# V from x·g with its rows scaled by the root afterwards, in a one-core decoder-layer kernel

## The chip, the core and the metric

The kernel runs on one core of a Trainium2 chip. The metric is the device time of one execution in microseconds. A core has TensorE (PE, with its weight loads PEld), VectorE (DVE), ScalarE (ACT), GpSimd (POOL) and SyncE (SP). Each works through its own instructions in the order of the program and waits on semaphores for the others. Here SP issues nearly all of the loads.

## What is computed

One layer of a decoder trunk, for one sequence of 1024 tokens of width 1024, in float32. Only the first sub-layer matters here:

```
mod = silu(c) @ w_ada + b_ada                        # shift, scale, gate (two sub-layers)
u   = (x * rsqrt(mean(x*x) + EPS)) * g_mix * (1 + scale) + shift
q, k, v, us, g_att, g_ssm = split(u @ w_in)
o_att = softmax over the dilated windows of q k^T, times v     # rows of the softmax sum to 1
...                                                  # S5 branch, gates, projection, conv MLP, final norm
```

Write g for g_mix·(1 + scale), one number for each channel, and r for the root rsqrt(...), one number for each token. Then u = r·(x·g) + shift, and u @ W = r·((x·g) @ W) + shift @ W.

## The kernel before, in words

Every float32 product is made of three matmuls on rounded halves: `mm3` (lines 182 to 186) multiplies high by high, high by low and low by high. A "split" writes the high half on ACT (a rounding copy) and then the low half on DVE (the difference). The work is laid out channel block by channel block, k = 0 to 7, 128 channels each; token halves are called hf = 0 and 1, 512 tokens each.

Stage one (lines 330 to 449) loads x transposed (`xs[k]`), the rows of w_ada that give the scale, and the first weights `w0`; DVE makes scale k with one row dot product (`row_dot`), ACT and DVE write x·g as two halves into a page `xg[k]`, and PE accumulates seven products of `w0` with xg in seven PSUM buffers `b0` (q and k of the first pair of heads and the inputs of the S5 branch). Meanwhile x is also loaded by tokens (`xn`), ACT sums its squares, and eight more row dots give the shift. `root` (line 388) makes r; `spread_a`, `spread_b` (lines 399 and 404) spread it over all partitions as `rr` with one matmul for each token half.

Between the stages (lines 452 to 507) PE multiplies the shift by `w0` (16 narrow matmuls, L488 and L489), and `u_half` begins to write u into new pages: for one k and one half, `u_a` is L1437 on DVE (x·g·r, in place in `xs`) and L1438 on ACT (high half of u), and `u_b` is L1443 on DVE (low half). `scale_r` (L462) multiplies the products in PSUM by rr and moves them into SBUF (`t0`).

Stage two (lines 566 to 609) makes v: for hf, for k, four token tiles t, one `mm3` each, with u as the stationary operand and w_v (`wv`, split by `split_w`, lines 301 to 306) as the moving one; eight PSUM buffers `vps`, four for each half. In the second half, around each k, DVE and ACT also turn `t0` into q and k of the first heads (`put_q`, `put_k`) and the finished first-half tiles into V (`put_v`: four copies L525 on ACT, four differences L528 on DVE). After the last product come `put_v(4)` to `put_v(7)`; the buffers `mm` that `put_v(4)` and `put_v(5)` read are the ones in which the next stage's first products are accumulated. The next stage is attention, with the remaining products of u as filling work for PE; before its first exponential, ACT copies the S5 inputs (L562) and loads its table.

The order on each engine is written by hand. `Builder` keeps a clock that `b.unit` moves on after each product; generators handed to `b.spawn` are resumed when that clock has passed the time that they last yielded, in the order in which they were spawned. `b.drain` runs them to their ends. `Weights` prefetches weight items the same way: its split is L118 on ACT and L121 on POOL.

## Time and profile before

| | before |
|---|---|
| median of 3 runs | 1157.44 us (1157.3 to 1157.76) |
| the profiled execution's own time | 1157.34 us |
| its span, first to last instruction | 1155.4 us |
| mean granted clock of TensorE | 0.986 |
| PE busy | 1112.6 us, 96% |
| DVE busy | 872.6 us, 76% |
| ACT busy | 581.8 us, 50% |

The span is the profiler's; the time of an execution is 1.94 us longer than it. The busy share of an engine is an average over stages that have different limits: what a change in one stage is worth is read from that stage's own timeline and waits.

### The profile page before, as it was taken

Reading aid. Unit: us, or ns where it says so; the run is one execution under the profiler, and the core shown is the slowest. Engines: PE = TensorE matmul, PEld = TensorE weight load, DVE = VectorE, ACT = ScalarE, POOL = GpSimd, SP = SyncE. Lnnn points to the kernel's source line nnn. Section 1 sums busy time; section 2 is a strip of 40 time slices with the busy share of each in tenths; the row PEclk is TensorE's granted clock in tenths of the full one; section 3 lists DMA queues with packets and bytes.
Section 4 is the critical chain, followed back from the end, with each engine's and each line's share of the span. In section 5 each row is a group of like instructions: output and inputs, shape, how many; then the busy total and the mean of one; then the engine's idle time right before and its main releaser. Section 6 shows DMA issues by size and latency. Waiting matters only on the chain.

```text
span 1155.4 us, 14755 instructions
## 1 busy us (share of the span) xinstructions
PE 1112.6 (96%) x5286; PEld 917.2 (79%) x5286; DVE 872.6 (76%) x1672; ACT 581.8 (50%) x1062; POOL 150.2 (13%) x171
## 2 busy tenths in 40 slices
PE   9899999999999999999799998999999999999995
PEld 8677888888878887888688886788888888887884
DVE  6678687876568597378767779888877768889777
ACT  3648777778732312242334565452445346736653
POOL 1001444545421312000000000000000000000003
PEclk9899999999999999999899999999999999999997
DMA  9811111111022221146592342255424337779333
GB/s 370 343 55 70 49 38 37 56 37 65 17 75 73 57 87 51 64 140 195 166 381 81 120 201 73 91 175 190 143 76 146 109 109 272 257 293 343 129 126 146
DMA packets 57337, 159.20 MB, mean 138 GB/s; under 512 B 7440, under 2 KB 13712, under 8 KB 55472
## 3 DMA queue, kind: packets, MB, share of 16 engines
q1 hardware_dynamic: 47520, 144.56, 35.1%
q10 hardware_dynamic: 9744, 13.70, 3.7%
q8 instruction: 41, 0.67, 0.2%
q14 instruction: 32, 0.26, 0.1%
HBM read 126.20 MB, written 31.46 MB: 136 GB/s over the span
## 4 chain that ended last, share of the span: by engine, by line
PE 66%; DVE 15%; ACT 8%; DMA 7%; issue 3%; POOL 0%; SPq 0%; DVEq 0%; ACTq 0%
PE ps_s L1305 13%; PE ps_mm L1305 10%; PE ps_t L1305 8%; PE ps_mm L184 6%; PE ps_mm L185 6%; PE ps_mm L186 6%; PE ps_s L186 3%; PE ps_s L184 3%; PE ps_s L185 3%; DMA xn<-in_xn 2%; PE ps_t L1598 2%; PE ps_s L1562 1%; PE ps_o L1615 1%; PE ps_s L1563 1%; DMA wraw<-in_w 1%
## 5 line engine op out<-in xcount | busy, mean ns | idle before, releaser
L1305 PE MATMUL ps_s<-op,half 128*128 128x512 f32 x792 | 189.5, 390 | 3.0 <-ACT ps_s L1319 2.4
L1305 PEld LDWEIGHTS ps_s<-op,half 128*128 128x128 f32 x792 | 148.4, 188 | 35.4 <-ACT ps_s L1319 3.8
L184 PE MATMUL ps_mm<-u,whl 128*128 128x512 f32 x360 | 145.0, 403 | 3.1 <-ACT sg L737 2.0
L186 PE MATMUL ps_mm<-u,whl 128*128 128x512 f32 x360 | 141.6, 393 | 0.0
L185 PE MATMUL ps_mm<-u,whl 128*128 128x512 f32 x360 | 141.4, 393 | 0.0
L1305 PE MATMUL ps_mm<-op,half 128*128 128x512 f32 x528 | 126.9, 393 | 3.0 <-DVE f L1010 2.8
L1305 PEld LDWEIGHTS ps_mm<-op,half 128*128 128x128 f32 x528 | 99.7, 189 | 24.6 <-ACT half L1110 3.2
L1305 PE MATMUL ps_t<-op,half 128*128 128x512 f32 x432 | 103.9, 390 | 0.7 <-ACT tp L1313 0.7
L1305 PEld LDWEIGHTS ps_t<-op,half 128*128 128x128 f32 x432 | 81.0, 188 | 17.9 <-ACT tp L1313 1.1
L1407 POOL TENSOR_TENSOR hh<-hh,acc 128x512 f32<-128x512 f32 x3 | 4.2, 1439 | 652.1 <-DVE acc L1432 652.1
L121 POOL TENSOR_TENSOR whl<-wraw,whl 128x256 fp32r<-128x256 f32 (+2 forms) x52 | 62.0, 1193 | 207.8 <-ACT whl L118 207.8
L184 PEld LDWEIGHTS ps_mm<-u,whl 128*128 128x128 f32 x360 | 68.1, 189 | 15.3 <-ACT sg L737 2.5
L186 PEld LDWEIGHTS ps_mm<-u,whl 128*128 128x128 f32 x360 | 68.0, 189 | 15.3 <-DVE whl L121 0.3
L185 PEld LDWEIGHTS ps_mm<-u,whl 128*128 128x128 f32 x360 | 68.3, 190 | 10.5
L1603 DVE TENSOR_TENSOR PT<-ps_t,PT 128x512 fp32r<-128x512 f32 (+1 forms) x80 | 50.6, 633 | 28.2 <-ACT PT L1601 27.7
L1111 DVE TENSOR_TENSOR half<-scr,half 128x512 fp32r<-128x512 f32 x80 | 54.5, 685 | 16.2 <-ACT half L1110 16.1
L118 ACT ACTIVATE whl<-wraw 128x256 fp32r<-128x256 f32 (+2 forms) x73 | 49.7, 681 | 28.3 <-PE ps_s L186 14.6
L1574 ACT ACTIVATE S<-S,mcol 128x128 f32<-128x128 f32 (+3 forms) x64 | 49.3, 771 | 14.5 <-DVE mcol L1572 13.0
L1578 POOL TENSOR_SCALAR S<-S,mcol 128x128 f32<-128x128 f32 (+3 forms) x64 | 48.6, 761 | 49.9 <-DVE mcol L1577 35.9
L1110 ACT ACTIVATE half<-scr 128x512 fp32r<-128x512 f32 x80 | 49.0, 626 | 8.6 <-DVE scr L1092 5.5
L1111 DVE TENSOR_TENSOR half<-wraw,half 128x512 fp32r<-128x512 f32 x66 | 45.0, 686 | 7.6 <-ACT half L1110 7.5
L1601 ACT ACTIVATE PT<-ps_t 128x512 fp32r<-128x512 f32 (+1 forms) x80 | 43.7, 550 | 10.4 <-PE ps_t L1598 9.3
(507 smaller groups left out, 2438.0 us busy)
## 6 DMA issues: line engine op xcount, KB each, us to landing
wraw<-in_wup SPq DMA_DIRECT2D x32, 512.0 KB, 3.7
fq<-f SPq DMA_DIRECT2D x16, 1024.0 KB, 5.4
ft<-fq SPq DMA_DIRECT2D x14, 1024.0 KB, 7.5
ada<-in_wada SPq DMA_DIRECT2D x24, 512.0 KB, 8.7
wraw<-in_wdn SPq DMA_DIRECT2D x20, 512.0 KB, 5.9
adaB<-in_wada ACTq DMA_DIRECT2D x16, 512.0 KB, 4.9
wraw<-in_wout SPq DMA_DIRECT2D x16, 512.0 KB, 3.9
hd<-h SPq DMA_DIRECT2D x12, 512.0 KB, 7.9
```

What stands on the lines that cost most here:

```text
L118: nc.scalar.activation(w[:, 0, cs], raw[:, cs], AF.Copy)
L121: lo.tensor_sub(w[:, 1, cs], raw[:, cs], w[:, 0, cs].bitcast(F32))
L184: nc.tensor.matmul(ps, wh, xh, start=first, stop=False)
L185: nc.tensor.matmul(ps, wh, xl, start=False, stop=False)
L186: nc.tensor.matmul(ps, wl, xh, start=False, stop=last)
L1110: nc.scalar.activation(w[:, 0], src, AF.Copy)
L1111: lows.append(lambda: nc.vector.tensor_sub(w[:, 1], src, w[:, 0].bitcast(F32)))
L1305: mm = lambda wp, xp, i: nc.tensor.matmul(ps, w[:, wp, ws], xp[:, cs], start=first and k + i == 0, stop=k == KT // 2 - 1 and i == 2, skip_ ...
L1574: nc.scalar.activation(tl, tl, AF.Exp, bias=mc[:, 0:1], scale=-1.0, accum_out=mc[:, 2:3])
L1578: nc.gpsimd.tensor_scalar(tl, tl, mc[:, 3:4], 0.0, op0=OP.mult, op1=OP.add)
L1601: nc.scalar.activation(pt[:, 0, :w], tps[:, :w], AF.Copy)
L1603: 0, lambda: nc.vector.tensor_sub(pt[:, 1, :w], tps[:, :w], pt[:, 0, :w].bitcast(F32)))
```

## The change

v is made of x·g instead of u: the second stage multiplies the pages `xg` that stage one left, so it needs no root; each row of the result is multiplied by r when it leaves PSUM (`put_v` takes it, from a new third row of `ssq`, as the scale of its copies and of its differences, which become `scalar_tensor_tensor`). The shift's part, shift @ w_v, is a constant row for each head; it is made by a second run of 16 narrow matmuls (`rows_of("v", wv)`) and eight small transposes, kept as `vb`, and added to the attention's output behind the softmax (line 1627's add becomes a `scalar_tensor_tensor` with that column).

u is still needed by the later products. It now takes the place of x·g in the same pages: `gen_u`, in the background, writes u for (k, hf) once the products of that k and half have been given (`taken`). The seven first products are copied out of PSUM on ACT as they end (`keep`) and scaled in SBUF later. Six of the eight row dots for the shift and their loads, the spreading of the root, and the shift's row for `w0` are moved into the second stage; the first w_v load and split are moved ahead into the first. `put_q`, `put_k` and `put_v` are spawned instead of being run in place.

```diff
...
@@ -50,7 +50,8 @@
 EPS = 1e-6
 BIG = 1e30
 WARM = 31
-DOTS = ((4, 5), (5, 1), (5, 4), (6, 0), (6, 2), (6, 4), (6, 6), (7, 1))
+DOTS = ((7, 1), (7, 4))
+U_PACE = 1.5
...
         def split_w(i):
             raw = raws.pop(i)
-            w = b.whl.tile([P, 2, 1024], R32, name="whl", tag="whl") if i == 5 else b.A([P, 2, 1024], R32, "whA")
+            w = b.whl.tile([P, 2, 1024], R32, name="whl", tag="whl") if i == 7 else b.A([P, 2, 1024], R32, "whA")
...
         def load_xn(n):
-            if n in (0, 2):
+            if n % 2 == 0:
                 page = b.A([P, 2, D], F32, "xn")
                 xnp[n], xnp[n + 1] = page[:, 0], page[:, 1]
-            nc.sync.dma_start(xnp[n % 4], I["xn"][n])
+            nc.sync.dma_start(xnp[n], I["xn"][n])
 
         def square(n):
 
-            nc.scalar.activation(xnp[n % 4], xnp[n % 4], AF.Square, accum_out=ssq[:, 0, n:n + 1])
+            x = xnp.pop(n)
+            nc.scalar.activation(x, x, AF.Square, accum_out=ssq[:, 0, n:n + 1])
...
+            nc.vector.tensor_scalar(ssq[:, 2], r, -1.0, None, op0=OP.mult)
...
+        def keep(i, ps):
+            if not t0_pages:
+                t0_pages.extend(b.A([P, 4, HF], F32, "t0") for _ in range(2))
+            t0[i] = t0_pages[i[0] // 2][:, 2 * (i[0] % 2) + i[1]]
+            nc.scalar.activation(t0[i], ps, AF.Copy)
+
         late = {}
-        for fn, at in ((row_dot, DOTS), (root, ((7, 0),)), (spread_a, ((7, 2),))):
+        for fn, at in ((row_dot, DOTS), (root, ((7, 2),))):
             for a, kn in enumerate(at):
                 late.setdefault(kn, []).insert(0, (fn, a))
...
-            if 3 <= k < 7:
-                load_row(2 * k - 6)
-                load_row(2 * k - 5)
-            if 2 <= k < 6:
-                for n in (2 * k - 4, 2 * k - 3):
-                    if n > 3:
-                        square(n - 4)
-                    load_xn(n)
+            for n in {2: (0, 1), 3: (2, 3), 4: (4, 5), 5: (6, 7)}.get(k, ()):
+                load_xn(n)
+            for n in {4: (0, 1), 5: (2, 3), 6: (4, 5)}.get(k, ()):
+                square(n)
+            if k == 5:
+                load_w(4)
+            for n in {5: (0, 1), 6: (2, 3)}.get(k, ()):
+                load_row(n)
             if k + 1 < KT:
                 prep_b(k + 1)
             if k + 2 < KT:
                 prep_a(k + 2)
             elif k == 6:
-                for n in range(4, KT):
+                for n in (6, 7):
                     square(n)
-                load_w(4)
+                wv = [split_w(4)]
                 load_w(5)
             o = (k % 2) * 512
             for n, ((t, hf), ps) in enumerate(b0.items()):
@@ -443,23 +455,23 @@
                 for fn, a in late.get((k, n), []):
                     fn(a)
                 b.mm3(ps, w[:, 0], w[:, 1], xg[k][:, 0, halves[hf]], xg[k][:, 1, halves[hf]], k == 0, k == KT - 1)
+                if k == KT - 1:
+                    keep((t, hf), ps)
                 b.unit(0.65)
-            del xg[k]
-        spread_b(0)
+        b0.clear()
+        del ps
         b.drain()
...
+        t0_pages.clear()
+        u = [xg[k] for k in range(KT)]
+        xg.clear()
 
         def scale_r(*ii):
             for i in ii:
-                nc.vector.tensor_mul(t0[i], b0.pop(i), rr[:, halves[i[1]]])
+                nc.vector.tensor_mul(t0[i], t0[i], rr[:, halves[i[1]]])
...
-        def u_half(k, hf, *between):
-            u_a(k, hf)
-            scale_r(*between)
-            u_b(k, hf)
...
+        taken = set()
+
+        def gen_u():
+
+            last = None
+            for hf in range(2):
+                for k in range(KT):
+                    while (k, hf) not in taken:
+                        yield 0.6
+                    u_a(k, hf)
+                    if last:
+                        u_b(*last)
+                    if last and last[1]:
+                        xs[last[0]] = None
+                    last = k, hf
+                    yield U_PACE
+            yield 0.7
+            u_b(*last)
+            xs[last[0]] = None
+
...
+        def shift():
+            nc.vector.tensor_add(mod[:, 0:KT], mod[:, 0:KT], cols[:, 0:KT])
+            nc.vector.tensor_copy(shl[:, :, 0], mod[:, 0:KT])
+            nc.vector.tensor_sub(shl[:, :, 1], mod[:, 0:KT], shl[:, :, 0].bitcast(F32))
+
+        def rows_of(n, ws, tag="o"):
+
+            ps = b.ps(tag)
+            for k in range(KT):
+                o = (k % 2) * 512
+                w = ws[k // 2][:, :, o:o + 512]
+                nc.tensor.matmul(ps[0:2], shl[:, k], w[:, 0], start=k == 0, stop=False)
+                nc.tensor.matmul(ps[0:1], shl[:, k, 0:1], w[:, 1], start=False, stop=k == KT - 1)
+                b.unit(0.43)
+            brow[n] = b.tp()
+            nc.scalar.activation(brow[n][0:2], ps[0:2], AF.Copy)
...
@@ -522,10 +549,11 @@
                 V.extend(b.A([P, 8, 2, P], R32, "V") for _ in range(4))
             src = vps[t].rearrange("p (h d) -> p h d", h=8)
             for p in range(4):
-                nc.scalar.activation(V[p][:, t, :, 0:HD], src[:, 2 * p:2 * p + 2], AF.Copy)
-            yield
+                nc.scalar.activation(V[p][:, t, :, 0:HD], src[:, 2 * p:2 * p + 2], AF.Copy, scale=ssq[:, 2, t:t + 1])
+            yield 0.7
             for p in range(4):
-                nc.vector.tensor_sub(V[p][:, t, :, HD:P], src[:, 2 * p:2 * p + 2], V[p][:, t, :, 0:HD].bitcast(F32))
+                nc.vector.scalar_tensor_tensor(V[p][:, t, :, HD:P], src[:, 2 * p:2 * p + 2], ssq[:, 2, t:t + 1],
+                                               V[p][:, t, :, 0:HD].bitcast(F32), op0=OP.mult, op1=OP.subtract)
...
         for hf in range(2):
             for k in range(KT):
                 if hf == 0:
-                    if k % 2 == 0 and k < 6:
-                        wv.append(split_w(5 + k // 2))
-                        if k == 0:
-                            load_w(7)
-                    if 1 < k + 1 < KT:
-                        u.append(b.A([P, 2, S], R32, "u"))
-                        u_half(k + 1, 0, *{3: [(1, 1)], 4: [(2, 1)], 5: [(0, 1)]}.get(k, []))
                     if k == 0:
+                        load_w(6)
+                        load_row(4)
+                        load_row(5)
+                        spread_a(0)
+                        row_dot(2)
+                        row_dot(3)
+                        wv.append(split_w(5))
+                    if k == 1:
+                        load_w(7)
+                        load_row(6)
+                        load_row(7)
+                        spread_b(0)
                         spread_a(1)
-                    if k == 1:
+                        row_dot(4)
+                        scale_r((1, 0))
+                        row_dot(5)
+                    if k == 2:
                         spread_b(1)
+                        wv.append(split_w(6))
+                        row_dot(6)
+                        scale_r((2, 0))
+                        row_dot(7)
+                        shift()
+                        b.spawn(gen_u(), 0.5)
+                    if k == 3:
+                        scale_r((0, 0))
+                    if k == 4:
+                        rows_of("u", w0)
+                        w0.clear()
+                        wv.append(split_w(7))
                     if k == 5:
-                        bias_cols()
+                        scale_r((3, 0), (1, 1))
+                        bias_cols("u", P, bias0)
+                    if k == 6:
+                        scale_r((2, 1))
+                        rows_of("v", wv)
                     if k == 7:
-                        u_half(0, 1)
-                        u_a(1, 1)
+                        scale_r((0, 1))
+                        bias_cols("v", HD, vb)
                 else:
                     if k == 0:
                         qk_tiles(0)
+                    if k in (2, 4):
+                        wv[k // 2 - 1] = None
                     put = put_q(0, k, add_bias0(0, k)) if k < 2 else put_k(0, k - 2, add_bias0(1, k - 2)) if k < 4 \
                         else put_v(k - 4)
-                    if k + 1 < KT:
-                        u_b(k + 1, 1)
-                    next(put)
-                    if k + 2 < KT:
-                        u_a(k + 2, 1)
-                    list(put)
-                    xs[k] = None
+                    b.spawn(put)
                     if k == 3:
                         us0 = [(t - 2, hf, add_bias0(t, hf)) for t, hf in ((2, 0), (2, 1), (3, 0))]
                     if k in (3, 6):
...
                     b.mm3(vps[t], u[k][:, 0, t * P:(t + 1) * P], u[k][:, 1, t * P:(t + 1) * P],
                           wv[k // 2][:, 0, o:o + 512], wv[k // 2][:, 1, o:o + 512], k == 0, k == KT - 1)
                     b.unit(0.65)
+                taken.add((k, hf))
             if hf == 0:
                 del xnp
                 vps += [b.ps(t) for t in ("mm", "mm", "o", "o")]
+        b.drain()
+        for t in range(4, 8):
+            list(put_v(t))
         p1.close()
         wv = None
         p2 = ExitStack()
...
         W.prefetch(1)
-        for t in range(4, 8):
-            list(put_v(t))
         for x in us0:
...
             hp = slice(64 * h2, 64 * h2 + 64)
             nc.scalar.activation(t[0:64, 0:256], o[64:128, 0:256], AF.Copy)
-            nc.vector.tensor_add(t[hp, 256:512], o[0:64, 0:256], t[0:64, 0:256])
+            nc.vector.scalar_tensor_tensor(t[hp, 256:512], o[0:64, 0:256], vb[0:64, 2 * p + h2:2 * p + h2 + 1], t[0:64, 0:256],
+                                           op0=OP.add, op1=OP.add)
             oo = Oat[p][hp, :, 2 * j * P:(2 * j + 2) * P]
```

## Rows read from the trace of the kernel before

**Rows 1.** The page, part 1: busy us, share of the span and instructions of each engine.

```profile
PE 1112.6 (96%) x5286; PEld 917.2 (79%) x5286; DVE 872.6 (76%) x1672; ACT 581.8 (50%) x1062; POOL 150.2 (13%) x171
```

**Rows 2.** Timeline of PE: start, us, line, operands, idle before with its releaser.

```profile
48.88 0.39 PE L186 MATMUL ps_o<-xg,whA 128*128 128x512 f32 x1
...
54.01 2.08 PE L407 MATMUL ps_o<-tp,nones 128*128 128x512 f32 x2 [4.74 <-ACT tp L402]
56.77 0.59 PE L488 MATMUL ps_o<-whl,shl 128*2 128x512 f32 x1 [0.69 <-ACT rr L408]
...
58.65 0.39 PE L489 MATMUL ps_o<-whl,shl 128*1 128x512 f32 x1
...
61.20 0.40 PE L184 MATMUL ps_s<-whA,u 128*128 128x512 f32 x1
...
65.48 1.02 PE L407 MATMUL ps_o<-tp,nones 128*128 128x512 f32 x2
...
77.32 0.40 PE L504 MATMUL ps_o<-ident,tp 2*128 2x2 f32 x4
...
108.33 0.39 PE L186 MATMUL ps_o<-whA,u 128*128 128x512 f32 x1
109.83 0.47 PE L184 MATMUL ps_mm<-u,whl 128*128 128x512 f32 x1 [1.10 <-DVE V L528]
```

**Rows 3.** Chain of work that ended last, first 55 us: start, us, what.

```profile
40.24 8.93 DMA xn<-in_xn
...
52.68 1.29 ACT tp L402 x4
```

**Rows 4.** Stretches: us, busy time (instructions) by engine, clock, DMA share, GB/s.

```profile
86.00:108.72 22.72, 22.24 (x97) 17.74 (x95) 20.11 (x41) 18.91 (x45) 3.73 (x2) 1.00 0.06 23
...
130.00:330.00 200.00, 196.85 (x1178) 168.68 (x1177) 139.91 (x407) 149.89 (x327) 93.22 (x124) 1.00 0.14 44
```

**Rows 5.** Timeline of DVE.

```profile
59.50 0.69 DVE L462 TENSOR_TENSOR t<-ps_s,rr 128x512 f32<-128x512 f32 x1
...
92.41 0.75 DVE L1437 SCALAR_TENSOR_TENSOR xk<-xk,gs,rr 128x512 f32<-128x512 f32 x1
93.08 0.67 DVE L551 TENSOR_TENSOR KL<-t,KH 64x512 fp32r<-64x512 f32 x1
...
94.47 0.42 DVE L555 CAST KH<-KH 64x512 fp32r<-64x512 f32 x1
...
101.80 1.54 DVE L1443 SCALAR_TENSOR_TENSOR u<-x,mod,u 128x512 fp32r<-128x512 f32 x1
...
108.00 0.89 DVE L528 TENSOR_TENSOR V<-ps_t,V 128x128 fp32r<-128x128 f32 x4 [1.65 <-ACT V L525]
108.80 1.67 DVE L528 TENSOR_TENSOR V<-ps_mm,V 128x128 fp32r<-128x128 f32 x8
```

**Rows 6.** Timeline of ACT.

```profile
9.50 0.61 ACT L379 ACTIVATE whl<-wvx 128x512 fp32r<-128x512 f32 x1
10.02 0.71 ACT L318 ACTIVATE xg<-xk,gs 128x512 fp32r<-128x512 f32 x1
...
100.23 0.74 ACT L525 ACTIVATE V<-ps_s 128x128 fp32r<-128x128 f32 x4
100.85 0.73 ACT L1438 ACTIVATE u<-x,mod 128x512 fp32r<-128x512 f32 x1
...
113.26 1.23 ACT L562 ACTIVATE usr<-t 128x512 f32<-128x512 f32 x1 [0.43 <-ACT usr L562]
```

**Rows 7.** Timeline of POOL.

```profile
100.41 2.39 POOL L121 TENSOR_TENSOR whl<-wraw,whl 128x1024 fp32r<-128x1024 f32 x1 [95.26 <-ACT whl L118]
```

**Rows 8.** Timeline of SP, the queue that issues the loads.

```profile
42.85 0.33 SPq L298 DMA_DIRECT2D wvx<-in_wv  x1
44.09 0.33 SPq L298 DMA_DIRECT2D wraw<-in_wv  x1
```

**Rows 9.** Line 1627 alone: its instructions, min/median/max ns, first and last start.

```profile
L1627 DVE TENSOR_TENSOR tp<-ps_o,tp x32: 406/417/419, 132.0 to 325.0; 64x256 f32<-64x256 f32 x32
```

More of the change, by code (lines that the diff above doesn't have):

```diff
@@ L566, in body @@
         vps = [b.ps(t) for t in ("s", "s", "t", "t")]
+        puts = []
         for hf in range(2):
@@ L687, in body @@
         W.slow = True
-        attention(b, V, QK, Oat, pS, near, far, ident, mcol, fill)
+        attention(b, V, QK, Oat, pS, near, far, ident, mcol, vb, fill)
         W.finish()
```

50 lines of the change are left out of this document (14 added, 36 removed).

## The prediction

> **What bounds the kernel now.** I read the busy shares first, then the chain that ended last, then the timelines of the first 125 us. Over the whole span TensorE is busy 96% of the time [rows 1], so nearly every us in which PE is kept waiting is a us of the result; the change acts only on the stretch from the end of the first products to the start of attention. The timeline of PE shows that stretch from both ends. The last first-stage product starts at 48.88, so the next could start at 49.1; it starts at 54.01, after 4.74 us of idleness, and the first product of V only at 61.20 [rows 2]. The chain says why: the last token block of x lands at 40.24 + 8.93 = 49.17, its root is spread by ACT at 52.68, and PE can only then spread it further [rows 3]. From 61.20 to the last product of V at 108.33 PE is nearly closed up, and after it waits once more, 1.10 us, for the low halves of V (L528), because the next products need the PSUM buffers that these still read; they start at 109.83 [rows 2]. So the quantity to be predicted is that 109.83. In the second half of V (86 to 108.7) DVE was busy 20.11 of 22.72 us [rows 4]: PE bounds the stretch, and DVE is close behind.
>
> **PE's part of the change.** The first product of V no longer waits for the root. What it needs is x·g, which is there, the first w_v tile, and free PSUM. The loads issue 1.24 us apart (42.85, 44.09 [rows 8]); the first w_v tile is moved ahead of eight row loads, so it lands some 10 us sooner, about 42, and its split (2 us) is done by 45. The second passes four row loads, lands about 48 to 49, and is split by 54.4, with PE at that tile at 55.5. The seven copies out of PSUM (`keep`) are ACT copies of 0.6 (as L379 in [rows 6]); the two that stand behind the root's chain on ACT are done at 48.9 and 49.4, and PE needs them at 50.5 and 51.2. Hidden, then; but the slack is 1 to 2 us, and beyond it each us is one of PE's. PE's work from 49.1 is: 192 products of V at 22.24/97 = 0.229 [rows 4], 44.0; 32 narrow products at (61.20 - 58.65)/11 = 0.232 [rows 2], 7.4 (16 of them new, for the shift's part of v); two spreads at 1.02, 2.0; twelve transposes at a quarter of 0.33 (the four at 77.32 [rows 2], the estimate from their row less the overlap), 1.0; and 1.5 allowed for waiting, mostly for the shift, which now comes behind six row dots and two low halves on DVE (63.2 against PE's 62). Sum 55.9, so V's products end at 105.0. That is 3.5 us before the 108.56 (108.33 + 0.229) of the kernel before, although PE has more to do.
>
> **DVE's part, which decides.** Before, u had to be written ahead of the products, and DVE entered the second half with most of it done. Now u may be written over x·g only behind the products: `gen_u` gives u(k, half) after they have been given. At the start of the second half (105.0 - 22.0 = 83.0) DVE has the last pieces of the first half and the whole second half of u ahead of it. It has nothing to do until about 80.7, when k = 6 of the first half has been released. From there to the low half of V's tile 4, which frees PE's next buffer, DVE's queue holds, in program order: 21 u steps at 0.67 (92.41 to 93.08 [rows 5]), 14.1; eight differences of q and k at 0.69 and four casts at 0.43, 7.2; five times four low halves of V at 0.80 (108.00 to 108.80), 4.0. Sum 25.3: without one wait, 106.0.
>
> To that come four terms. First, the low halves of V now take a column as their scale. A DVE instruction of 512 columns takes 0.75 with such a column (L1437) and 0.69 without (L462) [rows 5], so 20 instructions at 0.06 add 1.3 (0 if a short instruction hides it). Second, DVE waits in the q and k pieces: 1.1 for ACT copies that stand behind the high half of u(7, 0), which waits until PE has read what it overwrites, and 1.5 behind the four bias additions of k = 3. Third, a ring. From k = 4 on, DVE's order is L1437(k), L1443(k-1), low halves of V(j); ACT's order is L1438(k), copies of V(j). So the low halves wait for the copies, these for L1438, this for L1437, and the next L1437 stands behind the low halves. One turn is 0.75 + 0.63 (100.23 to 100.85 and like spacing) + 0.74 + 0.80 + two hops of 0.04 = 3.0 us with the durations of before [rows 5, 6]. A column as scale costs ACT 0.71 against 0.61 for 512 columns (L318, L379 [rows 6]): four copies make 0.74 into 1.10, and the turn 3.6. PE needs 12 x 0.229 = 2.75 for a k. Walked turn by turn DVE stands 0.8, 1.25, 1.25, 0.25 and 0.35, in sum 3.9 (2.5 with the old durations). Fourth, POOL. While L121 ran from 100.41 to 102.80 [rows 7], an L1443 that started at 101.80 took 1.54 and ended 0.54 behind it, against 0.75 otherwise; low halves of V, which read PSUM, were not longer. Two such splits now fall into DVE's queue. At the first, about 95.9, the next instruction is a cast, which would be held for 1.9; at the second the hold is 0 to 2.1, as an L1437 comes before or behind it; I take 0, since one that has begun isn't held.
>
> The Trainium skill (GPSIMD Engine Reference, Specifications) says that GpSimd shares its SBUF interfaces with VectorE and contends with instructions that have two SBUF inputs or run in a 2-port mode. By that rule both splits would hold DVE, and the result would be 2 us later than mine; the trace has one such case, of 0.79.
>
> Sum: 80.7 + 25.3 + 1.3 + 2.6 + 3.9 + 1.9 = 115.7, and PE comes back at 115.8, 6.0 later than before. (The same walk, with the order of the kernel before, puts that product at 110.0; the trace has 109.83.) With neither column, hold nor longer ring it is 80.7 + 25.3 + 2.6 + 2.5 = 111.1, still 1.3 later. PE has then been idle for 6 to 11 us. Behind the 4.74 us of before it ran at the lower of its two clocks: L407 took 2.08 instead of 1.02, and five narrow products from 56.77 to 58.65 took 1.88 instead of 1.16 [rows 2], 1.8 lost. That loss goes with the idle time of before and comes back here: PE is 7.8 late. ACT: the copies of V's tile 4 end at 114.6, three more tiles at 1.0 each and three L562 at 1.23 follow, 121.3 against 114.5 (113.26 + 1.23 [rows 6]), so the first exponential is 6.8 late.
>
> **Behind it.** In attention PE is busy 196.85 of 200 us [rows 4]: it has no room to catch up, and takes the delay over. Where ACT leads, the first us of PE's lateness is absorbed, so I take ACT's 6.8. The 32 additions at the end of each attention piece [rows 9] get a column too, at most 32 x 0.06 = 1.9 on a DVE that is idle for 60 of those 200 us: nothing, or at most that. One wait is added on ACT: the second prefetched weight item now shares its two buffers with the last w_v tile, and its split (L118) can't start before V ends; behind it on ACT are copies of V and high halves of u, but ACT comes to it at about 105 anyway: 0 to 0.3.
>
> Forecast: 1157.34 (the profiled execution, 0.10 below the median of 1157.44) + 6.8 = 1164.1.
>
> **Rivals.** *Faster.* DVE is not held by ACT: if the waits, holds and column prices of its queue come to under 3.7 us instead of 9.7, it is done before 109.7 and the delay turns into a gain. At best (106.0 plus 1.1 as before's last wait) PE is back at 107.1, 2.7 sooner: 1154.6. For it: DVE's floor is really 106.0, and before it bore 2.6 us of idleness in 22.7 without delaying PE. Against it: the ring is in the program order. *No change.* Short instructions hide the column, POOL holds nothing, and attention takes up the slower clock: 1.3 later, 1158.6 (up to 1160.5 with the clock). *The change doesn't do what it says,* because V's start still waits, for the second w_v tile or for the copies out of PSUM: one us late is one us of PE, and of everything that follows `taken`; 2 us would give 1166.1. It is on the slow side too.
>
> **How the numbers follow.** The slow forecast with its rivals on that side has 0.74, faster 0.12, no change 0.14. About 0.2% (2.3 us) is what a measurement of this kernel can tell from no change, so slower is above 1159.8 and faster below 1155.1. The upper bound adds the second hold (2.1), ACT's copies at the spacing of a longer instruction (0.8), PE's own lateness instead of ACT's (1.0) and some of the additions in attention: 1168.5. The lower end takes in the case of no change and reaches 1156.5; the part of the faster case below it is what is left out, with a little above the upper end.
>
> **What would show it.** Right: the first product of V starts at 49 to 50 without an idle time before it; V's last one near 105; L1437 for the last k starts several us behind it; PE then waits 6 to 11 us for L528 and runs its next products at twice their duration; L525 and L528 are 30% longer. Wrong: PE back before 109.8 (then the ring or DVE's sum is off), or a stall inside V's products (then the loads or the shift).

## The result, and the profile after

| | before | after |
|---|---|---|
| median, same chip | 1157.6 us (1157.3 to 1157.97, 4 runs) | 1169.08 us (1168.07 to 1169.97, 4 runs) |
| the profiled execution's own time | 1157.34 us | 1169.97 us |
| its span | 1155.4 us | 1168.2 us |

The ratio is 1.0099, with a 95% interval of 1.0081 to 1.0116: the changed kernel is slower by 11.5 us. The direction was forecast and the size was not: 6.8 us had been worked out, and the median lies 0.6 us above the range's upper end.

The timeline of PE in the changed kernel (start, us, line, operands, idle before with its releaser) answers [rows 2]; L185 to L187 are the three matmuls of a product, L410 spreads the root, L520 is the shift's row, L555 the low halves of V on DVE, L1613 the first score of attention:

```profile
48.90 0.39 PE L185 MATMUL ps_s<-whA,xg 128*128 128x512 f32 x1
...
51.86 1.13 PE L410 MATMUL ps_o<-tp,nones 128*128 128x512 f32 x2
...
63.00 0.40 PE L520 MATMUL ps_o<-whl,shl 128*2 128x512 f32 x1 [0.94 <-DVE shl L512]
...
104.02 0.39 PE L187 MATMUL ps_o<-whl,xg 128*128 128x512 f32 x1
117.36 0.76 PE L185 MATMUL ps_mm<-xg,whl 128*128 128x512 f32 x1 [12.95 <-DVE V L555]
117.92 0.63 PE L186 MATMUL ps_mm<-xg,whl 128*128 128x512 f32 x1
...
122.62 0.49 PE L185 MATMUL ps_mm<-xg,whl 128*128 128x512 f32 x1
...
123.40 0.22 PE L1613 MATMUL ps_s<-KH,QS 128*128 128x128 f32 x1
```

V starts at 48.90 instead of 61.20 and has no wait ahead of it; its last product starts at 104.02 instead of 108.33. All of that is lost in one place: 12.95 us of idle time before 117.36, ended by a low half of V on DVE. The twelve products behind it come 0.43 us apart. The stretches show the clock (us, then busy us and instructions of PE, PEld, DVE, ACT, POOL, then PE's granted clock, DMA share, GB/s):

```profile
86.00:104.30 18.30, 18.30 (x82) 14.91 (x80) 16.14 (x28) 12.54 (x25) 2.48 (x1) 1.00 0.09 29
104.30:108.00 3.70, 0.11 (x1) 0.00 (x0) 2.49 (x7) 2.69 (x6) 0.22 (x1) 1.00 0.00 0
108.00:117.30 9.30, 0.00 (x0) 0.00 (x0) 7.74 (x14) 4.74 (x16) 2.12 (x1) 0.56 0.27 85
117.30:122.70 5.40, 5.34 (x13) 4.21 (x14) 3.02 (x12) 4.97 (x11) 0.00 (x0) 0.50 0.20 41
122.70:130.00 7.30, 7.30 (x37) 6.19 (x36) 2.96 (x15) 4.97 (x12) 2.11 (x4) 0.99 0.31 117
```

It stood at 1.00 while V's products ran, fell during the idle time and was at 0.50, the lower of its two levels (1.2 GHz), from 117.3 to 122.7. The twelve products took 122.62 - 117.36 = 5.26 us instead of 12 x 0.229 = 2.75: 2.5 us lost.

What DVE did in those 13 us, and before, stands in its timeline. L1488 is `u_a`, L1494 `u_b`, L585 a cast of k, and the releaser L552 the copies of V on ACT:

```profile
95.79 2.53 DVE L585 CAST KH<-KH 64x512 fp32r<-64x512 f32 x1
...
103.13 1.13 DVE L555 SCALAR_TENSOR_TENSOR V<-ps_s,ssq,V 128x128 fp32r<-128x128 f32 x4 [0.78 <-ACT V L552]
104.17 0.74 DVE L1488 SCALAR_TENSOR_TENSOR xk<-xk,gs,rr 128x512 f32<-128x512 f32 x1
...
106.79 1.13 DVE L555 SCALAR_TENSOR_TENSOR V<-ps_t,ssq,V 128x128 fp32r<-128x128 f32 x4 [1.21 <-ACT V L552]
107.84 2.83 DVE L1488 SCALAR_TENSOR_TENSOR x<-x,gs,rr 128x512 f32<-128x512 f32 x1
...
112.49 1.13 DVE L555 SCALAR_TENSOR_TENSOR V<-ps_t,ssq,V 128x128 fp32r<-128x128 f32 x4 [1.16 <-ACT V L552]
...
116.09 2.16 DVE L555 SCALAR_TENSOR_TENSOR V<-ps_mm,ssq,V 128x128 fp32r<-128x128 f32 x8 [0.28 <-ACT V L552]
```

and POOL's two instructions of this time, the low halves of prefetched weights:

```profile
95.56 2.48 POOL L122 TENSOR_TENSOR whl<-wraw,whl 128x1024 fp32r<-128x1024 f32 x1 [90.41 <-ACT whl L119]
107.78 2.34 POOL L122 TENSOR_TENSOR whl<-wraw,whl 128x1024 fp32r<-128x1024 f32 x1 [9.75 <-ACT whl L119]
```

Two things eat DVE's time beside its work. It waits for ACT's copies of V once in each turn (0.78, 1.21, 1.16, 0.28). And two instructions lasted far too long (a hold, in what follows: the time that a DVE instruction takes beyond its usual time while POOL runs): the cast that began 0.23 us behind the first POOL split took 2.53 us (0.42 in [rows 5]), and the L1488 that began 0.06 us behind the second took 2.83 (0.74 otherwise). The second of these is the term that the prediction set at nothing.

ACT's side of the ring (L1489 writes the high half of u), and its first exponential (L1625), beside the kernel before's first score on PE and first exponential on ACT:

```profile
110.70 0.72 ACT L1489 ACTIVATE xg<-x,mod 128x512 fp32r<-128x512 f32 x1 [3.00 <-DVE x L1488]
...
124.11 0.40 ACT L1625 ACTIVATE S<-S,mcol 128x128 f32<-128x128 f32 x1
```

```profile
113.31 0.22 PE L1562 MATMUL ps_s<-KH,QS 128*128 128x128 f32 x1
...
115.81 0.40 ACT L1574 ACTIVATE S<-S,mcol 128x128 f32<-128x128 f32 x1
```

So PE entered attention 123.40 - 113.31 = 10.1 us late and ACT 124.11 - 115.81 = 8.3 us late.

### The profile page after: what moved, and what is told of

It is laid out like the page before. It is cut to its first block, busy times and chain, and to the rows that moved or that the text cites. A ratio compares the mean times of both kernels' runs of the same rounds, so it can differ in the third digit from the quotient of the medians.

```text
span 1168.2 us, 14831 instructions
## 1 busy us (share of the span) xinstructions
PE 1118.3 (96%) x5310; PEld 921.1 (79%) x5310; DVE 878.9 (75%) x1674; ACT 588.2 (50%) x1071; POOL 150.1 (13%) x171
## 4 chain that ended last, share of the span: by engine, by line
PE 71%; DVE 13%; ACT 8%; DMA 4%; issue 3%; SPq 0%; DVEq 0%; ACTq 0%
PE ps_s L1356 14%; PE ps_mm L1356 9%; PE ps_t L1356 8%; PE ps_mm L185 7%; PE ps_mm L187 7%; PE ps_mm L186 7%; PE ps_s L185 3%; PE ps_s L187 3%; PE ps_s L186 3%; PE ps_t L1649 2%; DMA ada<-in_wada 1%; PE ps_s L1613 1%; PE ps_o L1666 1%; PE ps_s L1614 1%; DVE op L920 1%
## 5 line engine op out<-in xcount | busy, mean ns | idle before, releaser
L185 PE MATMUL ps_mm<-xg,whl 128*128 128x512 f32 x368 | 148.9, 405 | 15.0 <-DVE V L555 12.9
L187 PE MATMUL ps_mm<-xg,whl 128*128 128x512 f32 x368 | 145.5, 395 | 0.0
L186 PE MATMUL ps_mm<-xg,whl 128*128 128x512 f32 x368 | 145.4, 395 | 0.0
L185 PEld LDWEIGHTS ps_mm<-xg,whl 128*128 128x128 f32 x368 | 70.4, 191 | 27.7 <-ACT V L552 13.3
L187 PEld LDWEIGHTS ps_mm<-xg,whl 128*128 128x128 f32 x368 | 70.0, 190 | 15.7 <-DVE whl L122 0.3
L186 PEld LDWEIGHTS ps_mm<-xg,whl 128*128 128x128 f32 x368 | 70.4, 191 | 11.1
L119 ACT ACTIVATE whl<-wraw 128x256 fp32r<-128x256 f32 (+2 forms) x73 | 49.8, 682 | 27.4 <-PE ps_s L187 14.7
L1625 ACT ACTIVATE S<-S,mcol 128x128 f32<-128x128 f32 (+3 forms) x64 | 49.3, 772 | 15.8 <-DVE mcol L1623 12.6
```

Of the source, the lines that this page charges most:

```text
L119: nc.scalar.activation(w[:, 0, cs], raw[:, cs], AF.Copy)
L185: nc.tensor.matmul(ps, wh, xh, start=first, stop=False)
L186: nc.tensor.matmul(ps, wh, xl, start=False, stop=False)
L187: nc.tensor.matmul(ps, wl, xh, start=False, stop=last)
L1625: nc.scalar.activation(tl, tl, AF.Exp, bias=mc[:, 0:1], scale=-1.0, accum_out=mc[:, 2:3])
```

## The experiments

The theory, after this reading: DVE's queue sets when PE comes back, and three separate terms lengthen it, POOL's holds, the ring with ACT and the column as scale. Behind it come the lower clock and the column in attention. The rivals: that these cover each other, so that taking one away only shows the next; and that attention takes over ACT's lateness, not PE's, as the prediction had it.

The runs were profiled one by one, and V began at 48.1 to 49.6 in them. So the table gives that start, PE's idle time before the next stage's first product, which doesn't depend on it, and the time from that product to the first score (3.48 in the kernel before, 113.31 - 109.83, for the same 15 products). Beside them stands the lateness against the kernel before at four points, which takes in V's start: the first score (start less 113.31), the first exponential (less 115.81), and the median over PE's instructions that started at 131 to 137 and at 295 to 303 in the kernel before.

| kernel | V begins | PE's wait | product to score | first score | first exponential | 131 to 137 | 295 to 303 | ratio (95%) |
|---|---|---|---|---|---|---|---|---|
| changed | 48.90 | 12.95 | 6.04 | 10.09 | 8.30 | 10.1 | 11.3 | 1.0099 (1.0081 to 1.0116) |
| second_hold | 49.43 | 10.98 | 6.25 | 8.85 | 7.73 | 8.8 | 9.7 | 1.0058 (1.0045 to 1.0072) |
| pool_away | 49.46 | 8.88 | 5.66 | 6.22 | 5.79 | 6.2 | 7.1 | 1.0051 (1.0037 to 1.0065) |
| v_ahead | 49.38 | 8.71 | 5.04 | 5.35 | 4.59 | 5.3 | 6.6 | 1.0049 (1.0036 to 1.0063) |
| both | 48.46 | 5.61 | 5.15 | 1.47 | 1.57 | 1.6 | 2.5 | 1.0022 (1.0011 to 1.0032) |
| no_column | 49.61 | 9.40 | 6.24 | 7.76 | 5.96 | 7.8 | 8.9 | 1.0074 (1.0061 to 1.0086) |
| warm_56 | 48.09 | 0.44 | 3.50 | 7.07 | 7.93 | 8.0 | 9.2 | 1.0075 (1.0063 to 1.0088) |
| plain_add | 48.15 | 12.95 | 5.58 | 8.87 | 7.58 | 8.8 | 8.9 | 1.0093 (1.0079 to 1.0107) |

### POOL's splits

`second_hold` takes the second split out of V's second half (first diff). `pool_away` takes out both and gives the first in the first half instead, the second behind V (second diff; its first lines stand in the first half):

```diff
-                    if k in (3, 6):
-                        W.prefetch(k // 3)
+                    if k == 3:
+                        W.prefetch(1)
```

```diff
                     if k == 6:
+                        W.prefetch(1)
                         scale_r((2, 1))
...
-                    if k in (3, 6):
-                        W.prefetch(k // 3)
```

> The changed kernel with the second weight split of the prefetch alone taken out of V's second half (it comes behind V, in attention's own pieces); the first stays where it is. This is the hold that the prediction set at nothing. Theory: the L1488 that took 2.83 us takes 0.74, the cast held by the first split still takes 2.5; PE comes back 2.1 sooner, at 115.3, ratio to the kernel before 1.008. Rival (DVE would have waited there for L1489 and V's copies anyway): PE back at 116.7 or later, ratio 1.0092 to 1.010.

> The changed kernel, with the two weight splits of the prefetch (L119 on ACT, L122 on POOL) taken out of DVE's crowded stretch: the first goes ahead of it (k = 6 of the first half), the second behind V. Theory (POOL holds DVE): in the changed kernel a cast that started 0.23 us behind the first split took 2.53 instead of 0.42 us, and an L1488 that started 0.06 behind the second took 2.83 instead of 0.74; each hold of 2.1 is paid in full, since DVE's chain sets when PE comes back. PE comes back at 113.2 instead of 117.36, time 1164.9. Rival (the holds lie in DVE's waits): DVE would then wait for ACT or PE instead, PE back at 116 or later, time 1167.5 to 1169.

PE's wait falls by 1.97 us with one split away and by 4.07 with both, where 2.1 and 4.2 were expected. In the DVE timeline of `second_hold` the first hold is still there, the second is gone, and the wait for ACT's copies behind it is as long as in the changed kernel (1.22 against 1.16):

```profile
96.31 2.53 DVE L585 CAST KH<-KH 64x512 fp32r<-64x512 f32 x1
...
108.36 0.74 DVE L1488 SCALAR_TENSOR_TENSOR x<-x,gs,rr 128x512 f32<-128x512 f32 x1
...
110.98 1.13 DVE L555 SCALAR_TENSOR_TENSOR V<-ps_t,ssq,V 128x128 fp32r<-128x128 f32 x4 [1.22 <-ACT V L552]
```

Each hold is paid nearly in full, and the rival falls. The measured ratios agree in sign; in size they are coarser than the traces: between `second_hold` and `pool_away` they show 0.0007 (0.8 us) where the waits differ by 2.1, and `second_hold`'s 1.0058 is lower than its trace explains, and lower than either expectation.

### The ring

```diff
-                    b.spawn(put)
+                    if k == 4:
+                        ahead = [put, put_v(1), put_v(2), put_v(3)]
+                        next(put)
+                    if 4 <= k < 7:
+                        next(ahead[k - 3])
+                    b.spawn(put if k < 4 else ahead[k - 4], 0.0 if k < 4 else 0.7)
```

> The changed kernel, with the copies of V (L552) issued one turn ahead on ACT, so that they no longer stand behind L1489 of the same turn: the ring L1488, L1489, L552, L555 is open. Theory (the ring): DVE's waits for L552 (0.78, 1.21, 1.16 and 0.28 us in the changed kernel, 3.4 in sum) go, a turn falls from 3.66 to DVE's own 2.6, PE comes back at 114.0 instead of 117.36, time 1165.7. Rival (DVE's sum and the products that L1489 waits for set the turn): the waits go over to L1489's wait for PE, PE back at 116.5 or later, time 1168 to 1169.

The wait falls by 4.24 us, where 3.4 were expected. DVE's three waits for the copies inside the ring are gone, 3.15; the last, 0.28, behind V's products, stays. The rest is half of the second hold, which changed its shape, in the timelines of DVE and POOL of this run (in which `u_a` is L1493 and `u_b` L1499):

```profile
106.37 0.74 DVE L1493 SCALAR_TENSOR_TENSOR x<-x,gs,rr 128x512 f32<-128x512 f32 x1
107.03 0.74 DVE L1499 SCALAR_TENSOR_TENSOR xg<-xk,mod,xg 128x512 fp32r<-128x512 f32 x1
107.69 1.12 DVE L555 SCALAR_TENSOR_TENSOR V<-ps_t,ssq,V 128x128 fp32r<-128x128 f32 x4
108.73 1.79 DVE L1493 SCALAR_TENSOR_TENSOR x<-x,gs,rr 128x512 f32<-128x512 f32 x1
```

```profile
106.59 3.38 POOL L122 TENSOR_TENSOR whl<-wraw,whl 128x1024 fp32r<-128x1024 f32 x1 [8.06 <-ACT whl L119]
```

Here DVE's u steps were running when POOL came, and POOL took 3.38 us instead of 2.34; the u_a at 108.73 ended 0.55 behind POOL's end at 109.97, 1.05 longer than usual. The one that had begun was not held; the other waited. But POOL, waiting since 106.59, also let the u_b of 107.03 pass, and by its length (109.97 - 2.34 = 107.63) it got its turn about when the low halves of V began.

Both moves together, the edits of `pool_away` and `v_ahead` in one kernel:

> The changed kernel with the two moves that were tried singly, together: the weight splits out of DVE's crowded stretch, and V's copies a turn ahead on ACT. Alone the first brought PE back at 113.87, the second at 113.62 (holds of 2.1 and 1.05 left in it), instead of 117.36. Theory (holds and ring are two separate terms of DVE's queue, and add up): PE back at 113.62 - 3.1 = 110.5; with the lower clock behind the wait still there, ratio to the kernel before 1.003. Rival (they cover the same time, and u's high halves, which wait for V's last products, are next): PE back at 112.5 or later, ratio 1.0045 or more.

The wait is 5.61: less by 7.34, of which 4.07 is the splits' share (as alone) and 3.27 the ring's (3.15 as read above). The terms add up, and PE is back at 109.63, about where the kernel before had it. The ratio is still 1.0022, because the lower clock (5.15 instead of 3.48 to the first score) and attention's column remain.

### The column

> The changed kernel, with V's copies and differences without the column as scale (L552 plain, L555 a tensor_sub, as in the kernel before): the rows of V are left unscaled, so this part of the computation is missing. Theory (the ring carries the column): L552 falls from 1.12 to 0.74 and L555 from 1.13 to 0.87 for four, a turn from 3.66 to 3.0; four turns and the last copies and differences give 3.1 us, PE comes back at 114.3 instead of 117.36, ratio to the kernel before 1.0073. Rival (the column hides in DVE's waits): PE back at 116.5 or later, ratio 1.009 to 1.010.

```diff
-                nc.scalar.activation(V[p][:, t, :, 0:HD], src[:, 2 * p:2 * p + 2], AF.Copy, scale=ssq[:, 2, t:t + 1])
+                nc.scalar.activation(V[p][:, t, :, 0:HD], src[:, 2 * p:2 * p + 2], AF.Copy)
...
-                nc.vector.scalar_tensor_tensor(V[p][:, t, :, HD:P], src[:, 2 * p:2 * p + 2], ssq[:, 2, t:t + 1],
-                                               V[p][:, t, :, 0:HD].bitcast(F32), op0=OP.mult, op1=OP.subtract)
+                nc.vector.tensor_sub(V[p][:, t, :, HD:P], src[:, 2 * p:2 * p + 2], V[p][:, t, :, 0:HD].bitcast(F32))
```

This kernel leaves the scaling of V's rows out. The wait falls by 3.55 us; DVE's four low halves take 0.88 us instead of 1.13, its waits in the ring fall to 0.42 and 0.85 (in this run `u_a` is L1487 and `u_b` L1493; POOL's row follows):

```profile
103.55 0.88 DVE L555 TENSOR_TENSOR V<-ps_s,V 128x128 fp32r<-128x128 f32 x4 [0.42 <-ACT V L552]
...
106.60 0.88 DVE L555 TENSOR_TENSOR V<-ps_t,V 128x128 fp32r<-128x128 f32 x4 [0.85 <-ACT V L552]
107.40 0.74 DVE L1487 SCALAR_TENSOR_TENSOR x<-x,gs,rr 128x512 f32<-128x512 f32 x1
108.06 2.83 DVE L1493 SCALAR_TENSOR_TENSOR xg<-xk,mod,xg 128x512 fp32r<-128x512 f32 x1
110.82 0.87 DVE L555 TENSOR_TENSOR V<-ps_t,V 128x128 fp32r<-128x128 f32 x4
```

```profile
107.59 2.75 POOL L122 TENSOR_TENSOR whl<-wraw,whl 128x1024 fp32r<-128x1024 f32 x1 [8.53 <-ACT whl L119]
```

The column isn't hidden: it is in the ring twice (ACT and DVE), as the prediction had it. Not all of the 3.55 is its price, though. With shorter low halves the u_a now began 0.19 us ahead of POOL and was not held, but the u_b behind it was, by 2.1 as in the changed kernel; ACT made its copies meanwhile, and the low halves at 110.82 have no wait. A wait like the 0.85 of the turn before is covered there, so that the column alone is worth about 2.7, an estimate.

This run also shows the second hold in the order that the prediction had counted on, `u_a` ahead of POOL: it falls on the next instruction and isn't smaller.

### The clock, and whose lateness counts

```diff
+        hot = b.ps("s")
+        for _ in range(56):
+            nc.tensor.matmul(hot[:, :P], b.nones, b.nones, start=True, stop=True)
         b.drain()
```

The first run had 76 in place of 56.

> The changed kernel, with 76 small matmuls (nones by nones, 0.16 us each by the row of L281, 12.1 us in sum) on PE in the stretch in which it waits; they write a PSUM buffer that nobody reads. Theory (PE's lateness is what attention takes over): the first twelve products behind the wait run at 0.23 instead of 0.43 us apart, 2.4 us are won, and the time falls by them to 1166.7. Rival (ACT's lateness is taken over, as the prediction had it): the first exponential stays at 124.1, since ACT comes to it only then, and the time stays at 1168.5 to 1169.1.

> As the run with 76 small matmuls in PE's waiting stretch, with 56. There each came as two passes of 0.111 us, so that the 76 lasted 16.9 us and kept PE from its products until 121.30, 3.9 us past the end of the wait; the products behind ran 0.23 apart. 56 of them last 12.4 us and end at 116.8. Theory (the lower clock behind the wait costs PE 2.5 us, and attention takes over PE's lateness): the first twelve products run 0.23 apart from 117.4, the time is 2.5 us below the changed kernel's, ratio to the kernel before 1.0077. Rival (attention takes over ACT's lateness, which this doesn't touch): ratio 1.0095 to 1.010.

The first run missed its aim: each small matmul came as two passes of 0.111 us, the 76 lasted 16.9 us and themselves kept PE busy until 121.3, and the ratio was 1.0099 (1.0083 to 1.0114), as without them. With 56 the PE timeline, and the stretch of the small matmuls (as above, the last three numbers are clock, DMA share and GB/s), read

```profile
103.77 12.67 PE L662 MATMUL ps_s<-nones 128*128 128x128 f32 x112
116.88 0.47 PE L185 MATMUL ps_mm<-xg,whl 128*128 128x512 f32 x1 [0.44 <-DVE V L555]
117.19 0.40 PE L186 MATMUL ps_mm<-xg,whl 128*128 128x512 f32 x1
...
128.96 0.50 PE L1616 MATMUL ps_s<-KH,QS 128*128 128x512 f32 x1 [0.77 <-DVE mcol L1619]
```

```profile
103.80:116.40 12.60, 12.60 (x113) 12.44 (x111) 9.83 (x19) 7.02 (x20) 2.35 (x1) 1.00 0.20 62
```

The clock stays at 1.00, the products run 0.23 apart at once (3.50 to the first score, 3.48 in the kernel before), and the ratio is the expected one. But the table tells more. In this run PE's first score is 7.07 us late and ACT's first exponential 7.93, and soon after PE is held for 0.77 us, by DVE behind ACT's exponentials, and is 8.0 late. In all eight rows the lateness at 131 to 137 is the larger of the two to within 0.1 us: PE's in six rows, ACT's in `warm_56` and `both`. Neither of the two theories was the whole: attention takes over the later of both. ACT's side of this rests on `warm_56` alone, since in `both` the two are 0.1 us apart. And it holds for this order of the work: in `fill_s` and `best_b` below, whose filling products are given elsewhere, the first exponential is 9.6 and 1.9 us late, and PE at 131 to 137 is 10.2 and 1.4.

### Attention's 32 additions

```diff
-            nc.vector.scalar_tensor_tensor(t[hp, 256:512], o[0:64, 0:256], vb[0:64, 2 * p + h2:2 * p + h2 + 1], t[0:64, 0:256],
-                                           op0=OP.add, op1=OP.add)
+            nc.vector.tensor_add(t[hp, 256:512], o[0:64, 0:256], t[0:64, 0:256])
```

> The changed kernel, with the 32 additions at the end of attention's pieces as tensor_add again, without the column vb: the shift's part of v is left out behind the softmax (it is still computed). In the changed kernel the lateness grew from 10.1 us at attention's start to 11.3 at its end. Theory (the column in these 32 costs it: 477 instead of 417 ns each, 1.9 us in sum at most): the lateness stays at 10.1 through attention, ratio 1.0088. Rival (the growth comes from elsewhere, as from the later start of the loads or a denser ACT): it grows by 1.2 us here too, ratio 1.0099.

The changed kernel's line 1678 alone, against [rows 9]:

```profile
L1678 DVE SCALAR_TENSOR_TENSOR tp<-ps_o,vb,tp x32: 467/477/480, 142.1 to 335.9; 64x256 f32<-64x256 f32 x32
```

This kernel leaves the shift's part of v out. It enters attention less late than the changed kernel because V began 0.75 us sooner and the stretch behind the wait took 0.46 less. From there the lateness stays (8.8, then 8.9); with the column it grows by 0.9 to 1.3 us in each of the other rows. The growth is the column's, 32 x 0.06 = 1.9 at most, of which half to two thirds arrive by 295 to 303. The ratio alone (1.0093) could not have told this.

Not all of the growth lasts. Behind attention, at 340 to 430, the lateness is 0.3 to 0.8 above that at 131 to 137 in the rows with the column (10.9 in the changed kernel) and 0.2 in `plain_add`. PE's busy time agrees, in the changed kernel and then in `plain_add` (196.85 in the kernel before [rows 4]): 0.5 us more of idleness with the column.

```profile
130.00:330.00 200.00, 196.35 (x1174) 167.74 (x1173) 145.50 (x420) 150.76 (x330) 93.61 (x125) 1.00 0.13 42
```

```profile
130.00:330.00 200.00, 196.85 (x1180) 168.42 (x1180) 143.27 (x418) 151.81 (x331) 93.62 (x125) 1.00 0.13 42
```

### Filling the wait with useful products, and a version beside the kernel before

```diff
-                    ps = b.ps("mm")
+                    first = p == 1 and j == 0 and hf == 0
+                    ps = b.ps("s" if first else "mm")
...
+        for _ in range(KT + 1):
+            b.unit(next(fill))
         W.slow = True
         attention(b, V, QK, Oat, pS, near, far, ident, mcol, vb, fill)
...
-    fills = 0
+    fills = KT
```

> The changed kernel, with the next stage's first group of 24 products accumulated in a PSUM buffer of the tag s, free since 104.2, instead of mm, and given whole ahead of attention: PE need not wait for V's tile 4 to begin it. Theory (PE's idle time is the loss, and attention takes it over us for us): 24 products of 0.229, 5.5 us, go into the 12.95 us of idle time; the time falls by 5.5 to 1163.6. Rival (attention is set by ACT or lacks this filling work at its end): under 2 us won, 1167 to 1169.

This came out at the rival's size, for another reason: 1168.28 us, 1.0083 (1.0069 to 1.0097). The 24 products did fit into the idle time, but PE then stood at the second score:

```profile
109.96 0.28 PE L1619 MATMUL ps_s<-KL,QS 128*128 128x128 f32 x1
121.08 0.58 PE L1618 MATMUL ps_s<-KH,QS 128*128 128x256 f32 x1 [10.85 <-DVE mcol L1621]
```

The first score's result is read on DVE behind all low halves of V, and the other buffer of this tag held the 24 products. DVE's queue, not the `mm` buffer, was the limit: moving PE's work ahead of it gains nothing until that queue is shorter. So the next runs shorten it (the edits of `pool_away` and `v_ahead`, those below, and, not shown, the addition for `vb` put behind the second half's start) and give the 24 products in the buffer `t`:

```diff
-            nc.vector.tensor_copy(kh[64:128, 0, hs], kh[0:64, 0, hs].bitcast(F32))
+            if p:
+                nc.vector.tensor_copy(kh[64:128, 0, hs], kh[0:64, 0, hs].bitcast(F32))
+            else:
+                nc.scalar.activation(kh[64:128, 0, hs], kh[0:64, 0, hs].bitcast(F32), AF.Copy)
...
-LEAD, FILL_PACE, SCORE_PACE = 9, 1.55, 1.2
+LEAD, FILL_PACE, SCORE_PACE = 9, 1.4216, 1.2
...
-        if want > 96:
-            want = 96 + (want - 96) / FILL_PACE * SLOW_PACE
+        if want > 88:
+            want = 88 + (want - 88) / FILL_PACE * SLOW_PACE
```

> The changed kernel with five things moved: the weight splits out of DVE's crowded stretch, V's copies one turn ahead on ACT, four casts of k from DVE to ACT, the addition for vb behind the second half's start, and the next stage's first 24 products in the buffer t (free by then), given whole ahead of attention, whose filling work is paced to last as long. Theory (DVE's queue at the end of V decides, and PE's start of the next stage is what attention takes over): the mm buffer is free before 109.8, PE works through from V's last product at 104.3, so that the next stage begins 5.5 us sooner than in the kernel before; attention's column takes 1.2 back: 4.3 us below the kernel before, ratio 0.9963. Rival (ACT, with V's copies, the four casts and the three copies L590 ahead of its first exponential, sets attention's start): first exponential at 119 against 115.8, ratio 1.000 to 1.002.

```diff
-            nc.scalar.activation(ur[m][:, :, hf * 64:(hf + 1) * 64], ps.rearrange("p (j t) -> p t j", t=T), AF.Copy)
+            out, src = ur[m][:, :, hf * 64:(hf + 1) * 64], ps.rearrange("p (j t) -> p t j", t=T)
+            if (m, hf) == (1, 1):
+                nc.scalar.activation(out, src, AF.Copy)
+            else:
+                nc.vector.tensor_copy(out, src)
```

> As the version with five things moved, which came out level with the kernel before, with ACT's work ahead of the first exponential made less: the three copies L590 go to DVE, idle there, and the next weight item's split comes behind the first 24 products. Theory (ACT sets attention's start there: first exponential at 117.73 against 115.81 before, PE waiting 2.45 us between 118 and 130 for DVE, whose queue waits for ACT's exponentials): first exponential at 114 to 115, those waits go, ratio 0.9975. Rival (attention lacks PE filling work, since 24 products have been given ahead, and runs at the pace of DVE and ACT): PE waits as much further on, ratio 0.9995 to 1.0005.

The first came out at 0.9998 (0.9989 to 1.0007), the rival's side: its first exponential was at 117.73, 1.9 us later than before. With three copies moved from ACT to DVE (and, not shown, one split later and one store issued by POOL instead of ACT) the exponential is at 115.55, and the median 1156.78 us, 0.9990 (0.9981 to 0.9999): 1.3 us below the kernel before's 1158.04, between the two expectations and less than the 0.2% that one would trust. PE starts the next stage 5 us sooner than before and keeps about 1 us of that: attention, which has 24 filling products less, waits longer for DVE than in the kernel before (PE is busy for 194.71 of the 200 us of [rows 4], against 196.85). Three such places in its PE timeline:

```profile
155.43 0.39 PE L1638 MATMUL ps_s<-KH,QS 128*128 128x256 f32 x1 [1.16 <-DVE mcol L1641]
...
160.50 0.52 PE L1674 MATMUL ps_t<-ident,S 128*128 128x128 f32 x3 [0.66 <-DVE mcol L1653]
...
163.12 0.63 PE L1674 MATMUL ps_t<-ident,S 128*128 128x128 f32 x4 [0.48 <-DVE mcol L1653]
```

A third run with the filling work distributed otherwise was worse:

```diff
-LEAD, FILL_PACE, SCORE_PACE = 9, 1.4216, 1.2
-SLOW_PACE, LAST_PACE, SLOW_END = 1.52, 0.5, 60
+LEAD, FILL_PACE, SCORE_PACE = 9, 1.55, 1.2
+SLOW_PACE, LAST_PACE, SLOW_END = 1.397, 0.5, 60
...
-        if want > 88:
-            want = 88 + (want - 88) / FILL_PACE * SLOW_PACE
+        if want > 62:
+            want = 62 + (want - 62) / FILL_PACE * SLOW_PACE
```

> As the version before it in this list, with attention's filling work given at the old pace (1.55 a step) in its first forty steps and thinner (1.397) behind, instead of thinner (1.42) in the first sixty. If a thin pace at the beginning is what makes PE wait there, the ratio is 0.001 lower than with the even pace; if the waits only move to where it is thin, it is the same.

It came to 1.0032 (1.0019 to 1.0044), worse than either side had it, with PE busy for 192.54 of the same 200 us: where the filling is thin PE waits, and giving it densely first made the thin part thinner.

## Why the prediction was wrong in size

- **PE's part held.** Start 49.1 foretold, 48.90 in the trace; no wait for copies or tiles; the wait for the shift 0.94 (of 1.5 allowed in all); V's products end at 104.25, foretold 105.0.
- **DVE's queue was right in its terms but for one, and in part by luck.** It starts at 80.1 (80.7 foretold). Waits in the q and k pieces 0.92 + 1.21 = 2.1 (2.6); ring 0.78 + 1.21 + 1.16 + 0.28 = 3.4 (3.9); first hold 2.1 (1.9); **second hold 2.1, taken as 0.** With the floor of 25.3 and 1.3 for the column (20 x 0.06 is 1.2) the sum is 116.4; PE came back at 117.36. Most of the 0.9 that is left is a turnover that I didn't price: an L1494 with another kind of instruction behind it takes 0.73 to 0.77 to the next start (90.68 to 91.44 in the trace), not the 0.67 of the sum. So start, waits and ring were 1.6 too long, first hold and turnovers 1.1 too short, and these nearly cancelled.
- **The failed step** is "at the second the hold is 0 to 2.1, as an L1437 comes before or behind it; I take 0, since one that has begun isn't held". The order was not open: in the five kernels that have this part as the changed one has it (changed, `warm`, `warm_56`, `plain_add`, `fill_s`) POOL was 0.05 to 0.06 us ahead, and the u_a took 2.83 to 2.88. Both follow the same copies on ACT, POOL behind the rounding of the weights (L119, 1.07), DVE behind four low halves (1.04). And the favourable order isn't free: the one that has begun isn't held, but in `no_column` the one behind it was, by 2.1, and in `v_ahead` a hold of 1.05 stayed. In no order that was measured did it come to nothing, so the hold belonged into the sum.
- **The rule of the Trainium skill was the better one.** The prediction weighed the Trainium skill's page GPSIMD Engine Reference, section Specifications, by which both splits would hold DVE (1166.1). The trace bears it out for both. The Trainium skill's page "SBUF — State Buffer", section "SBUF: two separate sides", adds the order: an exclusive lock, which whoever starts first has until its instruction ends, the other blocked; a DVE instruction is in it in a 2-port mode, or with two SBUF inputs against a GpSimd instruction that reads SBUF. `v_ahead` and `no_column` agree, from both sides (POOL 3.38 and 2.75 instead of 2.34, then a u step 1.79 and 2.83 instead of 0.74), and the low halves of V, with one input from PSUM, were not longer beside POOL (1.12). Which waiting instruction comes next when the first is done isn't settled: the u_b of 107.03 in `v_ahead` passed POOL, that of 108.06 in `no_column` didn't.
- **The clock was mis-sized:** 1.8 taken from the stall of before, behind 4.74 us of idleness; 2.5 here, behind 12.95. `warm_56` shows it by giving it back. Its size doesn't follow the length of the idle time: from the next stage's first product to the first score, 3.48 without a loss, it took 6.25 and 6.24 behind 10.98 and 9.40 us, 5.66 behind 8.88, 5.04 behind 8.71, 5.15 behind 5.61, and behind the same 12.95 us 6.04 in the changed kernel and 5.58 in `plain_add`. So it wanted a range, 1.6 to 2.8 in these runs, and the 0.7 lies within it.
- **"So I take ACT's 6.8" failed.** PE's 7.8 stood beside it, and the later one counts (table). That is 1.0 by the prediction's own numbers.
- **Attention's additions** were bounded at 0 to 1.9 and taken as nothing, since DVE is idle for 60 of 200 us. They cost 1.2 at 295 to 303 and 0.8 behind attention: PE waits longer even though DVE has room.

Together: 117.36 - 115.8 = 1.5 for PE's return, 0.7 for the clock, 1.0 for the choice of ACT, 0.8 for what lasts of attention's column, 4.0 of the 4.7 us between 6.8 and 11.5. The remaining 0.7 isn't assigned: behind attention the lateness moved by 0.5 to 2 us at about 450, 570 and 1060 us in the profiles, up in some runs and down in others (in the changed kernel from 10.9 to 12.0 at 570), and the profiled execution was the slowest of its four. The hold, the choice between PE and ACT, and attention had each been priced from both sides in the text, and each was then taken at its low end; the clock had one value only, and no bound. The upper end of the range added the hold and PE's lateness in full and 0.5 for attention; it had nothing for the clock's scatter, nor for what came behind attention.

The rival "faster" (DVE isn't held by ACT) falls: DVE waits 3.4 us for ACT's copies, and even `both`, without these waits (but for 0.28) and without POOL's holds, only comes back at 109.63, level with the kernel before. So does "the change doesn't do what it says": V does start without a wait.

## What to carry to other kernels

What work moved ahead on one engine is worth can't be told until the queue that follows on the other engines is walked too: here PE was done with V 4.3 us sooner and came back 7.5 us later, because DVE's queue could start only when its inputs might be overwritten. Walk such a queue in program order, with rings between engines as terms of their own, and where it hangs on which of two instructions starts first, take the hold and not its absence: ask also what comes behind the one that starts first. Give a term that was seen only once, as the clock's here, a range. When a stage is entered by two engines, compare both with the kernel before and carry over the later one.

## What the hardware showed beside this

The hold between DVE and POOL goes both ways: in `v_ahead` POOL's 2.34 us became 3.38, in `no_column` 2.75, with DVE first. In every case here the held DVE instruction ended soon behind POOL: 0.54 to 0.55 us for a u step, 0.28 for the cast. A column as scale costs a DVE instruction 0.06 us whatever its size here (0.477 against 0.417 for 64x256, 0.34 against 0.28 for 128x128), so that short instructions pay most for it in proportion. And small matmuls of 128x128 in f32 held the granted clock at 1.00 through 12.7 us in which PE had no other work (`warm_56`).
